# Attention's bias rows stored once and repeated from DRAM to DRAM in pieces of two heads, issued by GpSimd

## The chip, the cores and the metric

The kernel runs on one core of one Trainium2 chip. The metric is the time of one execution on the device in microseconds (us). A core has five engines with instruction queues of their own: TensorE (PE in the profile; its weight loads are PEld), VectorE (DVE), ScalarE (ACT), GpSimd (POOL) and SyncE (SP), and sixteen DMA engines that all queues share. SyncE, ScalarE and GpSimd issue transfers.

## The reference

One decoder layer over 2048 tokens of width 1024: a projection feeds eight RWKV-7 heads and eight heads of dilated attention, then an output product with layer norm, a mixture of 32 experts and a gated embedding with a second layer norm. The change concerns the attention's bias:

```python
def dilated_branch(q, k, v, rel_bias, window, dil):
    blk = window // dil                                  # 128 for each of the three patterns
    rel = np.arange(blk)[:, None] + blk - np.arange(2 * blk)[None, :]
    valid = ((rel >= 0) & (rel <= blk))[None] & (kpos >= 0)[:, None, :]
    bias = jnp.transpose(rel_bias[t5_bucket(np.clip(rel, 0, None) * dil)], (2, 0, 1))
    logits = jnp.einsum('bdhnqc,bdhnkc->bdhnqk', qs, kb) * (HEAD_DIM ** -0.5) + bias[None, None, :, None]
    logits = jnp.where(valid, logits, NEG_INF)
    ...
```

For a head and a pattern the bias of query i and key j depends only on i - j, so it is one row of 384 numbers, read with a shift of one for each query.

## The kernel before

The stages run one behind the other: `project` (the projection and what RWKV needs of it), `mixers` (RWKV and attention, woven together), `mix_out`, `route`, `ple`, `experts`, `finish`. The change lies in `attn_bias` (L953), a generator that `project` calls forward.

**What attn_bias makes.** For each of the three patterns GpSimd loads `hot` (which bucket each offset has, 32 x 384), the 32 x 8 table of `rel_bias` and `br` (8 x 384: the mask) (L960 to L962). A matmul (L965) looks the bias up for the eight heads, VectorE takes it from the mask (L966), and `br` then holds one row of 384 numbers for each head, in eight partitions. One transfer on ScalarE's queue (L967) writes each row 128 times to DRAM, into `biasrow` of 8 heads x 3 patterns x 128 x 384. In `attn_streams`, `load_bias` (L1002, SyncE) reads from there a tile in which row i is shifted by i, twelve times in all. `br` and `hot` have one buffer each, so the next pattern's loads wait until their readers are through.

**The loop in which it stands.** `project` holds TensorE's order by hand (`manual_schedule`); the other engines' order comes from a scheduler. The stretch is the loop over four column blocks `cc` and four token blocks `tb` (L478 to L486), in which every step does the same:

- `key(cc, tb)`: a product of 24 matmuls (L198 to L200) into one of five PSUM banks. ScalarE scales it into `sh` (L285), VectorE makes `o` (L287), SyncE stores `o` (L290), ScalarE squares `o` (L458).
- `value` twice: 24 shorter matmuls each. ScalarE copies the result into `ov` (L452), SyncE stores it to `va` (L453).
- between the two values `norm`: one matmul (L462) sums the square over each head. VectorE and ScalarE take the root and the reciprocal (L463 to L466), and SyncE stores the scaled key `rn` (L468).
- `next(bias)`: one yield of `attn_bias`.

`sh` and `ov` share the tag `"a"` of the pool `st`, which has two buffers, and are taken in the order `sh`, `ov`, `ov`. So a step's `sh` gets the buffer of the first `ov` of the step before, and L285 waits until its store to `va` has read it:

```python
sh = st.tile([P, BT + 1], F32, name="sh", tag="a")      # L283, in channels()
o = st.tile([P, 256], F32, name="ov", tag="a")          # L451, in value()
nc.scalar.copy(o, ps)
nc.sync.dma_start(self.va[t * P:(t + 1) * P, half * 256:(half + 1) * 256], o)
```

Behind L285 come L287, L458 and, in TensorE's fixed order, L462 with all that follows it. At the fourth step of a column block ScalarE also splits the next block's weights (L1230).

Four yields per pattern place the matmul of the patterns in steps 2, 6 and 10 of the loop, with the store behind it.

Of the kernel before, what the change touches and what calls it, by code (L numbers as in the profile page):

```python
# [18 lines left out]
P = 128  # L19
# [148 lines left out]
class K:  # L168
# [784 lines left out]
    def attn_bias(self, tile, bank):  # L953

        nc, I = self.nc, self.I
        L = 3 * P
        self.biasrow = rows = self.scratch("biasrow", (8, 3, P, L))
        for n in range(3):
            hot, br = tile(32, L + 8, "hot"), tile(8, L, "br")
            nc.gpsimd.dma_start(hot[:, 0:L], I["hot"][:, n])  # L960
            nc.gpsimd.dma_start(hot[:, L:], I["rel_bias"])
            nc.gpsimd.dma_start(br, I["gone"][:, n])  # L962
            yield
            ps = bank()
            nc.tensor.matmul(ps[0:8, 0:L], hot[:, L:], hot[:, 0:L], start=True, stop=True)  # L965
            nc.vector.tensor_tensor(out=br, in0=br, in1=ps[0:8, 0:L], op=ALU.subtract)  # L966
            nc.scalar.dma_start(rows[:, n], br.unsqueeze(1).to_broadcast([8, P, L]))  # L967
            yield
            yield
            yield  # L970

    def attn_open(self, es):
        self.al, self.ap = (es.enter_context(self.tc.tile_pool(name=name, bufs=1, reuse_waits="tile")) for name in ("al", "ap"))
# [1029 lines left out]
```

## Time and profile before

| | |
|---|---|
| median of three runs | 3235.52 us (3225.38 to 3244.79) |
| the profiled execution | 3237.51 us, of which the profile's span is 3235.7 us |
| VectorE busy | 2105.4 us (65%) |
| ScalarE busy | 1544.1 us (48%) |
| GpSimd busy | 628.3 us (19%) |
| TensorE's mean granted clock | 0.930 of full speed |
| moved by DMA | 533.09 MB, mean 165 GB/s |

Times within the span are counted from its start. A wait names an engine's instruction and what released it. [...] Transfers of SyncE and ScalarE have an issue time but no landing in the trace; those of GpSimd have both.

### The profile page before, as it was taken

Reading aid. Unit: us, or ns where it says so; the run is one execution under the profiler, and the core shown is the slowest. Engines: PE = TensorE matmul, PEld = TensorE weight load, DVE = VectorE, ACT = ScalarE, POOL = GpSimd, SP = SyncE. Lnnn points to the kernel's source line nnn. Section 1 sums busy time; section 2 is a strip of 40 time slices with the busy share of each in tenths; the row PEclk is TensorE's granted clock in tenths of the full one; section 3 lists DMA queues with packets and bytes.
Section 4 is the critical chain, followed back from the end, with each engine's and each line's share of the span. In section 5 each row is a group of like instructions: output and inputs, shape, how many; then the busy total and the mean of one; then the engine's idle time right before and its main releaser. Section 6 shows DMA issues by size and latency. Waiting matters only on the chain. (4 is left out here: it accounts for less than half of the span.)

```text
span 3235.7 us, 49913 instructions
## 1 busy us (share of the span) xinstructions
PE 2923.7 (90%) x17038; PEld 2331.5 (72%) x17039; DVE 2105.4 (65%) x4706; ACT 1544.1 (48%) x3704; POOL 628.3 (19%) x666
## 2 busy tenths in 40 slices
PE   7989888999799998999999799899999999999780
PEld 6666777777687777777787577788777777776560
DVE  4997333687564755656757678653577877775855
ACT  3444211465354454544544333311477777775754
POOL 0442000244110311211202122223011111111210
PEclk9999989999799888988997899999999999999895
DMA  5212433688725334235214453233499999997856
GB/s 172 76 56 95 104 89 79 197 276 265 160 62 109 112 81 113 83 83 117 81 29 134 143 179 131 98 129 100 165 295 314 327 311 311 327 299 236 284 155 214
DMA packets 364064, 533.09 MB, mean 165 GB/s; under 512 B 92376, under 2 KB 204640, under 8 KB 363792
## 3 DMA queue, kind: packets, MB, share of 16 engines
q1 hardware_dynamic: 330144, 459.09, 44.4%
q0 software_dynamic: 14496, 45.93, 6.0%
q10 hardware_dynamic: 19168, 24.86, 3.1%
q8 instruction: 136, 2.23, 0.3%
q14 instruction: 120, 0.98, 0.1%
HBM read 402.27 MB, written 128.06 MB: 164 GB/s over the span
## 5 line engine op out<-in xcount | busy, mean ns | idle before, releaser
L1711 DVE TENSOR_TENSOR wl<-raw,wh 128x512 fp32r<-128x512 f32 x768 | 478.3, 682 | 86.9 <-ACT wh L1710 86.5
L1710 ACT CAST wh<-raw 128x512 fp32r<-128x512 f32 x768 | 417.7, 621 | 12.9 <-DMA raw<-in_w_up_dram 10.0
L198 PE MATMUL ps<-xh,wh 128*128 128x512 f32 x640 | 261.3, 408 | 1.0 <-ACT xh L322 0.9
L199 PE MATMUL ps<-xl,wh 128*128 128x512 f32 x640 | 257.1, 402 | 1.2 <-DVE xl L323 1.2
L200 PE MATMUL ps<-xh,wl 128*128 128x512 f32 x640 | 256.6, 401 | 0.0
L1088 ACT ACTIVATE pe<-pe,ms 128x256 f32<-128x256 f32 (+1 forms) x384 | 174.9, 457 | 158.2 <-DVE ms L1085 144.7
L1840 POOL DMA_INDIRECT acc<-ysb,ix x48 | 95.1, 1981 | 622.1 <-ACT ysb L1839 401.4
L198 PE MATMUL pe<-wh,XX 128*128 128x512 f32 x480 | 198.8, 414 | 4.2 <-ACT wh L1710 4.2
L199 PE MATMUL pe<-wl,XX 128*128 128x512 f32 x480 | 191.1, 398 | 2.6 <-DVE wl L1711 2.6
L200 PE MATMUL pe<-wh,XX 128*128 128x512 f32 x480 | 189.9, 396 | 0.0
L198 PEld LDWEIGHTS ps<-xh,wh 128*128 128x128 f32 x640 | 123.9, 194 | 34.2 <-issue 2.8
L199 PEld LDWEIGHTS ps<-xl,wh 128*128 128x128 f32 x640 | 123.9, 194 | 29.8 <-DVE xl L323 2.4
L200 PEld LDWEIGHTS ps<-xh,wl 128*128 128x128 f32 x640 | 123.2, 192 | 29.2
L1094 PE MATMUL pl<-eye,pe 128*128 128x128 f32 x600 | 128.4, 307 | 13.7 <-ACT pe L1088 13.0
L1069 PE MATMUL pl<-KK,Q 128*128 128x256 f32 x432 | 117.4, 398 | 19.4 <-DMA KK<-ks 13.7
L1108 PE MATMUL po<-pe,V 128*64 128x128 f32 x1200 | 124.4, 313 | 8.5 <-DVE O L1122 6.7
L198 PE MATMUL pb<-gh,XH 128*128 128x512 f32 x320 | 126.4, 395 | 0.0
L199 PE MATMUL pb<-gl,XH 128*128 128x512 f32 x320 | 125.6, 393 | 0.0
L200 PE MATMUL pb<-gh,XL 128*128 128x512 f32 x320 | 125.4, 392 | 0.0
L1755 PE MATMUL pe<-wh,XX 128*128 128x512 f32 x288 | 119.9, 416 | 5.4 <-ACT wh L1710 5.4
L1756 PE MATMUL pe<-wl,XX 128*128 128x512 f32 x288 | 118.4, 411 | 2.9 <-DVE wl L1711 2.9
L1085 DVE CUSTOM_DVE_ANT_0 pe<-pl,bias 128x256 f32<-128x256 f32 x216 | 82.7, 419 | 56.4 <-PE pl L1069 38.6
(424 smaller groups left out, 7560.4 us busy)
## 6 DMA issues: line engine op xcount, KB each, us to landing
raw<-in_w_gate_dram SPq DMA_DIRECT2D x128, 512.0 KB
raw<-in_w_up_dram SPq DMA_DIRECT2D x128, 512.0 KB
raw<-in_w_down_dram SPq DMA_DIRECT2D x128, 512.0 KB
pk<-pk SPq DMA_DIRECT2D x32, 512.0 KB
pk_t<-pk SPq DMA_DIRECT2D x32, 512.0 KB
KK<-ks SPq DMA_DIRECT2D x64, 256.0 KB
wr<-in_w_in_dram SPq DMA_DIRECT2D x48, 256.0 KB
rkk<-rkk SPq DMA_DIRECT2D x32, 384.0 KB
```

Of the source, the lines that this page charges most:

```text
L198: mm(out, lh, rh, start=first, stop=False)
L199: mm(out, lh, rl, start=False, stop=False)
L200: mm(out, ll, rh, start=False, stop=last)
L1069: mm(pl[:, h], q, toks(KK[:, m, h], n, prev, 2), start=m == 0, stop=m == 1)
L1088: nc.scalar.activation(pe[:, h, w], pe[:, h, w], AF.Exp, bias=m_[h], scale=-1.0, accum_out=s_[h])
L1094: nc.tensor.transpose(pt[:, h, b], pe[:, h, b * P:(b + 1) * P], self.c("eye"))
L1108: mm(o[h * 64:(h + 1) * 64, j], vb[:, h * 64:(h + 1) * 64], tt[:, h, b], start=b == kb[0], stop=b == 1)
L1710: nc.scalar.copy(wh[:, c], raw[:, c])
L1711: nc.vector.tensor_tensor(out=wl[:, c], in0=raw[:, c], in1=wh.bitcast(F32)[:, c], op=ALU.subtract)
L1755: mm(ps, L[:, 0:P], wh, start=first, stop=False)
L1756: mm(ps, L[:, 0:P], wl, start=False, stop=last)
L1840: nc.gpsimd.indirect_dma_start(out=self.acc, out_offset=bass.IndirectOffsetOnAxis(ap=ix[0:r, e, b:b + 1], axis=0), in_=ysb[0:r], in_offset ...
```

## The change

A row of each head and pattern is first stored once (`biasone`, 8 x 3 x 384, 12 KB per pattern). Then four transfers per pattern, two heads each, read it from DRAM and write each row 128 times into `biasrow`. All five are issued by GpSimd, the old one by ScalarE. The number of yields per pattern is still four.

```diff
         self.biasrow = rows = self.scratch("biasrow", (8, 3, P, L))
+        one = self.scratch("biasone", (8, 3, L))
         for n in range(3):
...
             nc.vector.tensor_tensor(out=br, in0=br, in1=ps[0:8, 0:L], op=ALU.subtract)
-            nc.scalar.dma_start(rows[:, n], br.unsqueeze(1).to_broadcast([8, P, L]))
+            nc.gpsimd.dma_start(one[:, n], br)
             yield
-            yield
-            yield
+
+            for h in range(0, 8, 2):
+                nc.gpsimd.dma_start(rows[h:h + 2, n], one[h:h + 2, n].unsqueeze(1).to_broadcast([2, P, L]))
+                if h % 4:
+                    yield
```

In the built program TensorE, VectorE and SyncE have the same instructions in the same order as before, and ScalarE has them without the three stores. Lines from L958 on have other numbers in the changed kernel: by 1 up to its L967 (the subtraction), by 4 behind the loop. `hot`, `rel_bias` and `gone` are the loads of a pattern, `Lx` is the first work of the RWKV preparation behind the loop.

GpSimd, from the end of the token-shift work to the RWKV preparation, before:

```order
L363 TENSOR_TENSOR d<-X 128x512
L960 DMA hot<-in_hot_dram 32x384
L961 DMA hot<-in_rel_bias_dram 32x8
L962 DMA br<-in_gone_dram 8x384
L960 DMA hot<-in_hot_dram 32x384
L961 DMA hot<-in_rel_bias_dram 32x8
L962 DMA br<-in_gone_dram 8x384
L960 DMA hot<-in_hot_dram 32x384
L961 DMA hot<-in_rel_bias_dram 32x8
L962 DMA br<-in_gone_dram 8x384
L595 TENSOR_TENSOR Lx<-L 128x2x128
```

The same place of the changed kernel:

```order
L962 DMA hot<-in_rel_bias_dram 32x8
L968 DMA biasone<-br 8x384
L972 DMA biasrow<-biasone 2x128x384 x4
L963 DMA br<-in_gone_dram 8x384
L961 DMA hot<-in_hot_dram 32x384
L962 DMA hot<-in_rel_bias_dram 32x8
L968 DMA biasone<-br 8x384
L972 DMA biasrow<-biasone 2x128x384 x4
L963 DMA br<-in_gone_dram 8x384
L968 DMA biasone<-br 8x384
L972 DMA biasrow<-biasone 2x128x384 x4
L595 TENSOR_TENSOR Lx<-L 128x2x128
```

Each pattern's store and its four copies now stand in GpSimd's queue ahead of the next pattern's `br`.

ScalarE, around the first pattern's store, before:

```order
L464 ACTIVATE sq<-sq 128x512
L452 COPY ov<-ps 128x256
L967 DMA biasrow<-br 8x128x384
L285 ACTIVATE sh<-ps,prm 128x512
L458 ACTIVATE sq<-o,prm 128x512
```

The same place of the changed kernel:

```order
L464 ACTIVATE sq<-sq 128x512
L452 COPY ov<-ps 128x256
L285 ACTIVATE sh<-ps,prm 128x512
L458 ACTIVATE sq<-o,prm 128x512
L452 COPY ov<-ps 128x256
```

Only the store has left ScalarE's queue.

## Rows read from the trace of the kernel before

**Rows 1.** The page: busy time, share of the span and instructions of each engine.

```profile
PE 2923.7 (90%) x17038; PEld 2331.5 (72%) x17039; DVE 2105.4 (65%) x4706; ACT 1544.1 (48%) x3704; POOL 628.3 (19%) x666
```

**Rows 2.** Waits, 300 to 560 us: waiter <- releaser: total us, times, longest us.

```profile
POOL br L962 <- DMA biasrow<-br: 71.7, 2, 35.9
...
PE pn L462 <- ACT sq L458: 36.4, 3, 12.2
...
ACT sh L285 <- DMA va<-ov: 31.7, 3, 10.7
```

**Rows 3.** Windows from L462 to L462: us, busy by engine, clock, DMA share, GB/s.

```profile
378.01:402.42 24.41, 12.30 (x77) 10.56 (x75) 6.72 (x7) 3.93 (x7) 0.00 (x0) 0.82 0.51 78
402.42:417.00 14.58, 14.58 (x74) 12.49 (x75) 5.67 (x6) 2.79 (x5) 0.52 (x1) 0.83 0.36 108
442.27:466.61 24.34, 12.29 (x77) 10.56 (x75) 6.72 (x7) 3.93 (x7) 0.00 (x0) 0.84 0.51 79
466.61:481.49 14.88, 14.88 (x74) 12.79 (x75) 5.67 (x6) 2.79 (x5) 0.52 (x1) 0.81 0.38 113
...
506.70:531.22 24.52, 12.30 (x77) 10.56 (x75) 6.72 (x7) 3.93 (x7) 0.00 (x0) 0.84 0.51 77
531.22:546.20 14.98, 14.98 (x74) 12.89 (x75) 5.67 (x6) 2.80 (x5) 0.00 (x0) 0.80 0.36 112
...
558.33:570.46 12.13, 12.13 (x77) 10.60 (x76) 5.62 (x6) 2.79 (x5) 0.00 (x0) 1.00 0.18 65
570.46:583.12 12.66, 12.29 (x77) 10.55 (x75) 6.77 (x7) 3.89 (x8) 0.00 (x0) 1.00 0.25 79
```

**Rows 4.** The same view of the first long step, cut where TensorE stops.

```profile
378.01:390.20 12.19, 12.19 (x76) 10.55 (x74) 4.04 (x2) 2.52 (x5) 0.00 (x0) 1.00 0.53 82
390.20:402.42 12.22, 0.11 (x2) 0.01 (x1) 2.68 (x5) 1.41 (x2) 0.00 (x0) 0.65 0.50 75
```

**Rows 5.** Timeline of ScalarE: start, us, instruction, [idle before <- releaser].

```profile
371.22 0.55 ACTq L967 DMA_DIRECT2D biasrow<-br  x1
...
398.91 0.69 ACT L285 ACTIVATE sh<-ps,prm 128x512 f32<-128x512 f32 x1 [10.52 <-DMA va<-ov]
...
580.75 0.68 ACT L285 ACTIVATE sh<-ps,prm 128x512 f32<-128x512 f32 x1
```

**Rows 6.** Timeline of SyncE's queue, the two stores of that step in one row.

```profile
378.65 7.40 SPq L453 DMA_DIRECT2D va<-ov  x2
```

**Rows 7.** Timeline of GpSimd.

```profile
406.67 0.52 POOL L962 DMA_DIRECT2D br<-in_gone_dram  x1 [35.82 <-DMA biasrow<-br]
434.08 0.52 POOL L960 DMA_DIRECT2D hot<-in_hot_dram  x1 [26.89 <-PE ps L965]
...
600.18 0.62 POOL L595 TENSOR_TENSOR Lx<-L 128x256 f32<-128x256 f32 x1 [128.69 <-DVE L L591]
```

**Rows 8.** DMA queues (packets, MB, share of 16 engines) and one issue (KB each).

```profile
q1 hardware_dynamic: 330144, 459.09, 44.4%
q0 software_dynamic: 14496, 45.93, 6.0%
...
biasrow<-br ACTq DMA_DIRECT2D x3, 1536.0 KB
```

**Rows 9.** Timeline of VectorE.

```profile
367.37 3.35 DVE L466 RECIPROCAL rn<-sq 128x512 f32<-128x512 f32 x1 [0.70 <-ACT sq L464]
...
370.65 0.53 DVE L966 TENSOR_TENSOR br<-br,ps 8x384 f32<-8x384 f32 x1
```

**Rows 10.** GpSimd's issues: `br` in the DMA view (us to landing), slot tables (ns min/median/max).

```profile
br<-in_gone_dram POOLq DMA_DIRECT2D x3, 12.0 KB, 2.4
...
L1643 POOL DMA_DIRECT2D sl<-slotlist x4: 584/1298/1778, 2230.4 to 2239.0; - x4
```

**Rows 11.** The instructions of L1002: ns min/median/max, first and last start.

```profile
L1002 SPq DMA_DIRECT2D bias<-biasrow x12: 360/371/537, 813.2 to 1558.4; - x12
```

## The prediction

> **What bounds the kernel now.** TensorE is busy 2923.7 of 3235.7 us [rows 1], so time is won where it stands still or runs at a low clock. The change touches only the place where the attention bias is written, so I read that stretch: first who waits for whom between 300 and 560 us [rows 2]. TensorE has one wait worth naming there: three times, 36.4 us in all, its matmul L462 waits for ScalarE's square. Just above stands the reason: ScalarE's L285 waits three times for `va<-ov`, a store of 128 KB that holds a buffer of the tag that L285 writes next. And GpSimd waits twice for `biasrow<-br`, 35.8 us each.
>
> Next the stretch cut at each start of L462 on TensorE [rows 3]. A step of this loop takes 12.13 us (558.33 to 570.46), and the fourth step of a column block takes 12.66 (570.46 to 583.12). But the fourth steps that follow a bias store take 24.41, 24.34 and 24.52 us, and the steps after them 14.58, 14.88 and 14.98. In [rows 4] the first long step is cut in two: until 390.20 TensorE is full, then it does nothing for 12.2 us. The DMA share is 0.50 in that half, where a normal step has 0.18: eight of sixteen DMA engines are held. The store's eight heads take one engine each. After the idle time the step at 402.42 has a granted clock of 0.83: 17% of 14.58 us is 2.5 us, just what this step is longer than 12.13. [...]
>
> The order of events is in the timelines. The bias store is issued at 371.22 [rows 5] and lets `br` go at 406.67 [rows 7]: 35.45 us for 1536 KB [rows 8], 44 GB/s, 5.5 GB/s for each of eight engines. `va` is issued at 378.65 [rows 6] and L285, which waits for it, starts at 398.91 [rows 5], so `va` landed 20 us after its issue, when 27.7 of 35.45 us (78%) of the bias store were over.
>
> **What the losses are worth.** Long steps against 12.66: 11.75 + 11.68 + 11.86 = 35.29 us. Steps behind them against 12.13: 2.45 + 2.75 + 2.85 = 8.05 us. Together **43.3 us**, the most that the change can give back here.
>
> **The change part by part.** *Removed:* three issues on ScalarE's queue, 0.27 to 0.55 us each, while ScalarE is busy 3.93 of 24.41 us [rows 3]: nothing. *Added:* for each of three patterns one store of 12 KB and four copies of 384 KB, all on GpSimd. The order of TensorE, VectorE, ScalarE and SyncE is otherwise the same. On GpSimd the next row behind the last copies is L595 at 600.18 [rows 7], with 128.69 us idle ahead of it; between the copies stand only small loads for the next pattern, and GpSimd now idles 26.89 us behind the second pattern's `br` load until that pattern's matmul [rows 7]. GpSimd's issues cost nothing while this cover stands. The wait added is that the first copy follows the landing of the 12 KB store, and only those loads queue behind it. The reader of the bias, L1002, first issues at 813.2 [rows 11], some 300 us after the third pattern.
>
> *The price of the copies* is the open term: the bytes are the same, but they are read from DRAM, where the old store read eight SBUF partitions. No long DRAM-to-DRAM copy is timed in this trace. Bounds from [rows 8], over 16 x 3235.7 = 51771 engine-us: q1 moves 459.09 MB in 44.4% of it, 20.0 GB/s per engine; GpSimd's own queue q0 moves 45.93 MB in 6.0%, 14.8 GB/s; the old bias store 5.5 GB/s. For 1.573 MB on eight engines these hold the engines for 9.8, 13.3 and 35.4 us. I take **13.3**: it is the queue that the copies use, and a source of many rows in DRAM is more like its traffic than like eight partitions of SBUF. On sixteen engines it would be half.
>
> *Does `va` then land in time?* VectorE's subtraction L966 ends at 370.65 + 0.53 = 371.2 [rows 9]. Issue of the 12 KB store 0.5 us and landing 2.4 us, as for the load of the same size [rows 10], then 0.7 us for the first copy's issue: copies run from about 374.8. With the same 78% `va` lands at 374.8 + 0.78 x 13.3 = 385.2. It is needed when L285 starts in an undisturbed fourth step: 580.75 [rows 5] is 10.29 us behind that step's start, so 378.01 + 10.29 = 388.3. **It lands 3 us early and the stall is gone**, and with it the stretch at the low clock. The limit is a hold of (388.3 - 374.8) / 0.78 = 17.3 us; of each us above it 0.78 us come back as stall, and then about 2.7 us of clock per bias.
>
> *The issues.* Four loads of a slot table, the nearest issues on GpSimd with many pieces, take 0.58 to 1.78 us each [rows 10]. At 1.78 the last copy comes 7.1 us after the first; should it hold `va` as the first does, `va` lands at 392.3, 4.0 us late: 3 x (4.0 + 2.7) = 20 us lost again. This is the far end for this case.
>
> [...]
>
> **Sum.** 3237.5 us for the profiled execution (span 3235.7, 1.8 around it) - 43.3 = 3194.2. The median of the three runs is 2.0 below the profiled execution: **3192 us**. Everything behind 583 us starts 43 us earlier in the same order.
>
> **Rivals.**
> *The engines are held as long as before.* The price may lie in writing 3072 short rows to DRAM rather than in the source; then the hold stays 35.4 us and begins 3.6 us later, `va` lands at 402.4, and three stalls grow by 3.5 us: 3235.5 + 10.6 = 3246, within what can be told from no change. For it: the write side is unchanged. Against it: q1's mean of 20 GB/s includes many stores. [...]
> *A part of the stall stays,* with a hold between 17.3 and 31 us. At 25 us `va` is 6.0 us late: 3 x (6.0 + 2.7) = 26 us are lost again, 3218.
> *Two engines carry all four copies* (the slower side). A copy of two heads can use two engines, as eight heads used eight. Should all four land on the same two, 1.573 MB at 2 x 14.8 GB/s holds these for 53.1 us; `va` needs them too and lands 374.8 + 41.4 = 416.2, 17.3 us later than now, three times: 3287. It decides from a hold of 30.9 us, 25 GB/s per engine, above both measured rates; at 20.0 it is 3255. Against it: nothing in the trace shows that GpSimd's queue prefers certain engines. [...]
>
> **How the numbers follow.** A difference below 0.5% (16 us) can't be told from no change here, since the three runs span 19 us. Stall gone 0.76 (its own range 3180 to 3212: the runs' spread below, the issues' far end above); a part left 0.09; held as before 0.08; two engines 0.07. Faster by over 0.5% means below 3219: 0.76 and half of the second, 0.81. Slower by over 0.5% is the two-engine case, 0.07. The rest, 0.12, is within. The range is 3179 to 3224: the first case and most of the second.
>
> **What would show it.** Right: L462 waits for ScalarE once, below 1 us; all fourth steps near 12.7 us and those behind near 12.1 at clock 1.00; L285 waits for no `va`; `br`'s second load waits for the 12 KB store only, a few us. The copies' hold shows in the DMA share of the steps: about 0.5 more for some 13 us. Wrong: long steps remain (held as before, or two engines, told apart by a share raised by 0.50 or by 0.13), or the steps are short and the time is lost behind 583 us.

## The result, and the profile after

The changed kernel takes **3195.79 us** (median of six runs, 3188.58 to 3220.28), the kernel before 3238.43 in the runs beside it: a ratio of **0.9879 [0.9851, 0.9908]** with its 95% interval (taken over all runs, so not quite the quotient of the medians, 0.9868). The forecast was 3192. The profiled span is 3192.6 us against 3235.7.

The page of the changed kernel, busy time by engine, answers to [rows 1]:

```profile
span 3192.6 us, 49926 instructions
...
PE 2910.0 (91%) x17038; PEld 2320.6 (73%) x17039; DVE 2098.2 (66%) x4706; ACT 1541.6 (48%) x3704; POOL 641.5 (20%) x681
```

The kernel is 43 us shorter with the same matmuls. To see where, the span of each kernel is cut at the first and the last L462 of the loop (columns as in [rows 3]: us; busy time of PE, PEld, DVE, ACT and POOL, each with its number of instructions; the granted TensorE clock as a share of full speed, a mean over the stretch; the mean busy share of the sixteen DMA engines; GB/s). Before:

```profile
352.80:583.12 230.32, 193.57 (x1119) 165.73 (x1117) 89.99 (x97) 47.69 (x85) 3.08 (x6) 0.91 0.35 81
583.12:3235.70 2652.58, 2417.70 (x14626) 1928.67 (x14626) 1759.31 (x4236) 1354.86 (x3379) 526.22 (x588) 0.93 0.58 180
```

After, with two of the three fourth steps that follow a bias, one step behind and the last fourth step, from L462 to L462, which answer to [rows 3]:

```profile
354.10:541.34 187.24, 185.77 (x1118) 159.62 (x1116) 90.10 (x97) 47.01 (x85) 17.72 (x21) 1.00 0.32 100
541.34:3192.60 2651.26, 2408.90 (x14626) 1921.19 (x14626) 1752.16 (x4236) 1352.90 (x3379) 524.39 (x588) 0.93 0.58 180
...
379.32:391.97 12.65, 12.29 (x76) 10.55 (x74) 6.81 (x7) 3.88 (x8) 0.36 (x1) 1.00 0.66 188
391.97:404.20 12.23, 12.23 (x74) 10.70 (x75) 5.62 (x6) 2.63 (x5) 0.00 (x0) 1.00 0.33 108
...
479.52:492.18 12.66, 12.29 (x76) 10.56 (x74) 6.82 (x7) 3.88 (x8) 0.00 (x0) 1.00 0.64 188
...
528.68:541.34 12.66, 12.29 (x76) 10.55 (x74) 6.76 (x7) 3.88 (x8) 0.00 (x0) 1.00 0.26 84
```

The loop gave 230.32 - 187.24 = 43.08 us, the 2650 us behind it 1.3, and the part ahead of it takes 1.3 more. Its granted clock went from 0.91 to 1.00, and the bias still moves: GpSimd is busy 17.72 us in it instead of 3.08. The steps of 24.4 us are gone (the third fourth step not shown here takes 12.66), and a step with a bias behind it (share 0.66) takes as long as the one without (share 0.26). The waits between 300 and 560 us, in place of [rows 2]:

```profile
DVE sh L284 <- DMA va<-ov: 8.8, 3, 3.0
...
POOL biasrow L972 <- DMA biasone<-br: 4.6, 3, 1.5
...
PE pn L462 <- ACT sq L458: 1.5, 4, 0.4
```

L462 waits 1.5 us in all instead of 36.4. The store `va` is still waited for, by VectorE's small copy L284 into the same `sh`, but 3.0 us at most, with nothing late behind it. In the kernel before, that copy waited too:

```profile
DVE sh L284 <- DMA va<-ov: 46.3, 6, 15.2
```

GpSimd's timeline, the copies' row of the DMA view (last number: median us to landing) and SyncE's:

```profile
372.79 0.52 POOL L968 DMA_DIRECT2D biasone<-br  x1 [0.64 <-DVE br L967]
374.81 4.34 POOL L972 DMA_DIRECT2D biasrow<-biasone  x4 [1.50 <-DMA biasone<-br]
```

```profile
biasrow<-biasone POOLq DMA_DIRECT2D x12, 384.0 KB, 13.6
```

```profile
379.96 4.04 SPq L453 DMA_DIRECT2D va<-ov  x2
```

And VectorE's and ScalarE's rows that tell when `va` was in, and when it was needed:

```profile
388.06 0.15 DVE L284 COPY sh<-edge 128x1 f32<-128x1 f32 x1 [2.94 <-DMA va<-ov]
```

```profile
389.61 0.68 ACT L285 ACTIVATE sh<-ps,prm 128x512 f32<-128x512 f32 x1
```

The copies' first issue started at 374.81 and they took 13.6 us each (forecast 13.3). `va` landed at 388.06, 8.1 us after its issue instead of 20, and ScalarE's L285 used it at 389.61, 1.5 us later; 3.1 were forecast. But L285 isn't the first that needs it. In VectorE's queue stand L284, the scaling of `rn` (L467), the rest of the weights' split (L1235) and L287, in this order:

```profile
389.21 1.29 DVE L1235 TENSOR_TENSOR wl<-wr,wh 128x512 fp32r<-128x512 f32 x2 [0.34 <-ACT wh L1234]
390.42 0.74 DVE L287 SCALAR_TENSOR_TENSOR o<-ps,prm,sh 128x512 f32<-128x512 f32 x1
```

Only the 0.34 us that VectorE idles ahead of L1235 stand between a later `va` and a later L287, for which the square L458 and L462 wait. The margin is some 0.4 us, as experiment 10 shows.

### The profile page after: what moved, and what is told of

Read it like the earlier page. It is cut to its first block, busy times and chain, and to the rows that moved or that the text cites. A ratio compares the mean times of both kernels' runs of the same rounds, so it can differ in the third digit from the quotient of the medians.

```text
span 3192.6 us, 49926 instructions
## 1 busy us (share of the span) xinstructions
PE 2910.0 (91%) x17038; PEld 2320.6 (73%) x17039; DVE 2098.2 (66%) x4706; ACT 1541.6 (48%) x3704; POOL 641.5 (20%) x681
## 5 line engine op out<-in xcount | busy, mean ns | idle before, releaser
L1714 ACT CAST wh<-raw 128x512 fp32r<-128x512 f32 x768 | 417.3, 620 | 12.4 <-DMA raw<-in_w_up_dram 10.4
L1098 PE MATMUL pl<-eye,pe 128*128 128x128 f32 x600 | 127.5, 306 | 12.4 <-ACT pe L1092 12.1
L1089 DVE CUSTOM_DVE_ANT_0 pe<-pl,bias 128x256 f32<-128x256 f32 x216 | 82.6, 419 | 49.7 <-PE pl L1073 36.4
```

What stands on the lines that cost most here:

```text
L1098: nc.tensor.transpose(pt[:, h, b], pe[:, h, b * P:(b + 1) * P], self.c("eye"))
L1714: nc.scalar.copy(wh[:, c], raw[:, c])
```

## The experiments

The change does three things at once: GpSimd issues instead of ScalarE, the source is DRAM instead of SBUF, and one transfer becomes four. The theories: **source** (reading each row from DRAM makes the store quick), **issuer** and **pieces**. All ratios are against the kernel before, run on the same chip beside each. All but experiments 8 and 9 keep the engines' order apart from the edited transfers (in 6 and 11 a few of VectorE's instructions trade places; in 9 and 11 L467 comes ahead of L284). The *hold* is the time for which a bias transfer keeps its DMA engines.

### 1. The issuer alone

```diff
-            nc.scalar.dma_start(rows[:, n], br.unsqueeze(1).to_broadcast([8, P, L]))
+            nc.gpsimd.dma_start(rows[:, n], br.unsqueeze(1).to_broadcast([8, P, L]))
```

> Only the issuer changes: the old store of eight heads, read from eight SBUF partitions, is issued by GpSimd instead of ScalarE. Source theory (the price of a row lies in its eight-partition SBUF source): GpSimd's second load of br still waits 33 to 38 us, the three fourth steps stay at 22 to 27 us, and the time is that of the kernel before, ratio 0.995 to 1.005. Issuer theory (GpSimd's queue lets the store to va through): fourth steps of 12.7 us and a ratio near 0.988.

Measured: 1.0065 [1.0037, 1.0094], slower. First the window of the first fourth step, then the DMA view, SyncE, and ScalarE's L285:

```profile
378.04:409.86 31.82, 12.29 (x77) 10.55 (x75) 6.72 (x7) 3.98 (x8) 0.54 (x1) 0.75 0.49 70
```

```profile
biasrow<-br POOLq DMA_DIRECT2D x3, 1536.0 KB, 35.3
```

```profile
378.68 7.14 SPq L453 DMA_DIRECT2D va<-ov  x2
```

```profile
406.35 0.69 ACT L285 ACTIVATE sh<-ps,prm 128x512 f32<-128x512 f32 x1 [17.93 <-DMA va<-ov]
```

The store takes 35.3 us as before, so the issuer gave nothing of the gain. It costs something: `va` landed at 406.35, just ahead of the bias store's end, and not at 398.91 [rows 5]. The three fourth steps (31.82, 31.14, 31.20) are 20.9 us longer in sum than in [rows 3], which is the 0.65%; neither theory had this loss.

### 2. The source alone

```diff
-            nc.scalar.dma_start(rows[:, n], br.unsqueeze(1).to_broadcast([8, P, L]))
+            nc.gpsimd.dma_start(one[:, n], br)
             yield
+            nc.scalar.dma_start(rows[:, n], one[:, n].unsqueeze(1).to_broadcast([8, P, L]))
...
```

> Only the source changes: the 12 KB are stored once, and one transfer of eight heads, issued by ScalarE, repeats them from DRAM to DRAM. Source theory: eight engines are held for 10 to 14 us instead of 35, the fourth steps take 12.6 to 13 us, ratio 0.985 to 0.990. Issuer theory: fourth steps of 22 to 27 us, ratio near 1.000. Pieces theory (transfers of two heads let the store to va in between them): also near 1.000.

Measured: 0.9878 [0.9818, 0.9939], the whole gain. The window of the first fourth step, SyncE's store, and VectorE's L284:

```profile
377.96:390.62 12.66, 12.29 (x76) 10.56 (x74) 6.82 (x7) 3.88 (x8) 0.00 (x0) 1.00 0.45 157
```

```profile
378.61 4.04 SPq L453 DMA_DIRECT2D va<-ov  x2
```

```profile
384.51 0.15 DVE L284 COPY sh<-edge 128x1 f32<-128x1 f32 x1 [0.75 <-DMA va<-ov]
```

With ScalarE as issuer and eight heads in one transfer, `va` is in after 5.9 us and the stall is gone. ScalarE's queue (q10 in the DMA view) has its last packets of the bias before 385.1, a hold of 11.9 us from the issue at 373.18. The rival "held as before", by which the writing of short rows sets the price, falls: the rows written are the same.

### 3. The pieces alone

The old source, in four transfers of two heads by GpSimd:

```diff
-            nc.scalar.dma_start(rows[:, n], br.unsqueeze(1).to_broadcast([8, P, L]))
...
+            for h in range(0, 8, 2):
+                nc.gpsimd.dma_start(rows[h:h + 2, n], br[h:h + 2].unsqueeze(1).to_broadcast([2, P, L]))
...
```

> Issuer and pieces change, the source does not: four transfers of two heads, issued by GpSimd, read from br in SBUF. Source theory: the hold stays 33 to 38 us, fourth steps of 22 to 27 us, ratio 0.995 to 1.005. Pieces theory: fourth steps near 12.7 us, ratio near 0.988.

Measured: 1.0070 [1.0041, 1.0099]. Fourth steps 31.84, 35.17 and 31.74 us. The first, and the DMA view:

```profile
377.56:409.40 31.84, 12.29 (x76) 10.56 (x74) 6.72 (x7) 3.93 (x7) 0.00 (x0) 0.73 0.51 64
```

```profile
biasrow<-br POOLq DMA_DIRECT2D x12, 384.0 KB, 39.4
```

A quarter of the bytes, read from two partitions, takes 39.4 us while the others run beside it. The pieces theory falls from this side. Hold and steps lie above what the source theory gave; the steps are near those of experiment 1, with the same issuer.

### 4. One piece, otherwise as changed

```diff
-            for h in range(0, 8, 2):
-                nc.gpsimd.dma_start(rows[h:h + 2, n], one[h:h + 2, n].unsqueeze(1).to_broadcast([2, P, L]))
+            nc.gpsimd.dma_start(rows[:, n], one[:, n].unsqueeze(1).to_broadcast([8, P, L]))
```

> As the changed kernel, but one transfer of eight heads per pattern instead of four of two. Source theory: landing after 12 to 17 us, fourth steps of 12.6 to 13 us, ratio 0.985 to 0.990, the same as the changed kernel. Pieces theory: the store to va waits behind the one large transfer, fourth steps above 15 us, ratio above 0.991.

Measured: 0.9887 [0.9857, 0.9917], fourth steps 12.66 us. DMA view, SyncE and VectorE:

```profile
biasrow<-biasone POOLq DMA_DIRECT2D x3, 1536.0 KB, 12.4
```

```profile
377.86 4.04 SPq L453 DMA_DIRECT2D va<-ov  x2
```

```profile
385.20 0.15 DVE L284 COPY sh<-edge 128x1 f32<-128x1 f32 x1 [2.18 <-DMA va<-ov]
```

The pieces theory falls from this side too. All 1536 KB land in 12.4 us, and this is the plain price that the forecast put at 13.3.

### 5. Why SBUF was slow: the same rows, spread over partitions

The source stays in SBUF and ScalarE issues one transfer, but the heads stand in partitions 0, 4, ... 28 instead of 0 to 7 (the matmul then has 32 output rows, and GpSimd first clears what the loads leave unwritten).

```diff
-            nc.tensor.matmul(ps[0:8, 0:L], hot[:, L:], hot[:, 0:L], start=True, stop=True)
+            nc.tensor.matmul(ps[0:32, 0:L], hot[:, L:], hot[:, 0:L], start=True, stop=True)
...
-            nc.scalar.dma_start(rows[:, n], br.unsqueeze(1).to_broadcast([8, P, L]))
+            nc.scalar.dma_start(rows[:, n], br[0:32:4].unsqueeze(1).to_broadcast([8, P, L]))
```

> The source stays SBUF and ScalarE issues one transfer as before, but the eight heads lie in partitions 0, 4, 8 to 28 instead of 0 to 7. Partition-group theory (the old store was slow because eight neighbouring partitions share a narrow way out): the hold falls to 9 to 15 us, fourth steps near 12.7 us, ratio 0.985 to 0.990. Rival (each engine is slow because all its rows come from one partition): the hold stays 33 to 38 us and the ratio is 0.995 to 1.005. [...]

Measured: 0.9841 [0.9781, 0.9902]. ScalarE's issue, the release of `br` on GpSimd, and the fourth step:

```profile
373.58 1.28 ACTq L969 DMA_DIRECT2D biasrow<-br  x1
```

```profile
384.57 0.41 POOL L961 MEMSET br<- 32x384 f32 x1 [11.42 <-DMA biasrow<-br]
```

```profile
380.40:393.06 12.66, 12.29 (x77) 10.55 (x75) 6.77 (x7) 3.88 (x8) 0.93 (x2) 1.00 0.35 124
```

The hold is 11.0 us instead of 35.45, with the bytes, rows and issuer unchanged. So "SBUF against DRAM" was not the cause either: eight *neighbouring* partitions were. With the heads four partitions apart the store runs at 143 GB/s instead of 44, 3.2 times the rate. Why neighbouring partitions are slow was not shown.

### 6. The wait moved: buffers of its own for `ov`

The old store is left alone; `ov` gets two buffers outside tag `"a"` (lines behind it move by one).

```diff
-                        o = st.tile([P, 256], F32, name="ov", tag="a")
+                        o = vo.tile([P, 256], F32, name="ov", tag="v")
```

> The bias store stays as in the kernel before; instead ov gets two buffers of its own, so that L285 waits for no store to va (sq has one buffer less, to make room). Buffer theory (the stall comes only through the shared tag): the hold stays near 35 us, the fourth steps fall to 12.6 to 14 us, ratio 0.985 to 0.991. Rival (the held engines stop TensorE in other ways too, by the stores of o and rn or the weight loads): fourth steps above 18 us, ratio above 0.993.

Measured: 0.9903 [0.9880, 0.9926]. Waits between 340 and 600 us, and the fourth step with the one behind:

```profile
POOL br L963 <- DMA biasrow<-br: 73.3, 2, 36.6
ACT ov L453 <- DMA va<-ov: 46.9, 9, 8.4
```

```profile
376.83:389.49 12.66, 12.29 (x76) 10.55 (x74) 6.75 (x6) 3.83 (x7) 0.00 (x0) 1.00 0.54 88
389.49:404.65 15.16, 12.40 (x75) 10.66 (x75) 5.76 (x6) 2.59 (x5) 0.00 (x0) 1.00 0.53 95
```

The engines are held as long as before (GpSimd waits 36.6 us for the bias store, 35.9 in [rows 2]), yet most of the loss is gone. That shows the chain: it ran through the shared buffer, from `va` to L285. The rest waits at `ov`'s own buffer: steps behind of 15.16, 15.14 + 13.76 and 14.89 + 13.84 us are 12.1 us above five times 12.13, and 43.3 - 12.1 = 31.2 us is 0.96%, where 0.97% was measured.

### 7. All sixteen engines

Each row is stored twice, and one GpSimd transfer per pattern repeats sixteen rows 64 times. The first two dimensions of `biasrow` and `biasone` trade places for it.

```diff
-            nc.gpsimd.dma_start(one[:, n], br)
+            nc.gpsimd.dma_start(one[n], br.unsqueeze(1).to_broadcast([8, 2, L]))
...
+            nc.gpsimd.dma_start(rows[n].rearrange("h (t i) l -> (h t) i l", t=2), one[n].rearrange("h t l -> (h t) l").unsqueeze(1).to_broadcast([16, P // 2, L]))
```

> As the changed kernel, but each row is stored twice and one transfer with an outer dimension of sixteen repeats it, so that sixteen engines can share it. Engine-count theory (an engine moves 15 GB/s, so the hold goes with the rows of one engine): landing after 6 to 9 us instead of 13.5, the store to va lands 2 to 5 us after its issue instead of 8, and the ratio is again 0.985 to 0.990, since no stall was left. Rival (DRAM is the limit): landing still 12 to 15 us.

Measured: 0.9876 [0.9853, 0.9899]. Windows of 2 us (last columns: clock, DMA share, GB/s):

```profile
379.00:381.00 2.00, 2.00 (x20) 2.00 (x19) 1.30 (x2) 0.63 (x1) 0.00 (x0) 1.00 0.96 327
381.00:383.00 2.00, 2.00 (x14) 1.73 (x13) 2.00 (x1) 0.37 (x1) 0.00 (x0) 1.00 0.28 97
```

The engines are full until 381 and then free: the share from 374.8 to 381 is 0.87, at 291 GB/s. So the hold falls to some 6 us, and DRAM wasn't the limit at 12.4. `va` is in by 383.60, 5.1 us after its issue at 378.52 (5.5 in the second pattern). No time comes of it. With the stall gone there is nothing left to gain here, as the forecast's bound of 43.3 us says.

### 8. The four pieces, issued by ScalarE

```diff
-                nc.gpsimd.dma_start(rows[h:h + 2, n], one[h:h + 2, n].unsqueeze(1).to_broadcast([2, P, L]))
+                nc.scalar.dma_start(rows[h:h + 2, n], one[h:h + 2, n].unsqueeze(1).to_broadcast([2, P, L]))
```

> The four DRAM-to-DRAM copies of two heads are issued by ScalarE instead of GpSimd. The order of the mixers' stage changes in this build, so the steps of the loop decide, not the total. Two-engine theory (this queue puts all four copies on the same two engines): the DMA share rises by about 0.13 for some 50 us per pattern, and fourth steps take 30 to 45 us. Eight-engine theory: share up by 0.5 for 10 to 14 us, fourth steps of 12.6 to 13 us.

Measured: 1.0073 [1.0050, 1.0095], slower, but not by the expected route. A window while TensorE stands still, the long step, and ScalarE's timeline:

```profile
381.00:385.00 4.00, 0.00 (x0) 0.00 (x0) 0.00 (x0) 0.00 (x0) 0.00 (x0) 0.50 0.13 50
...
364.74:393.29 28.55, 13.25 (x78) 10.71 (x77) 5.98 (x7) 2.84 (x6) 2.03 (x4) 0.78 0.19 66
```

```profile
376.07 16.40 ACTq L972 DMA_DIRECT2D biasrow<-biasone  x2
392.52 0.72 ACT L458 ACTIVATE sq<-o,prm 128x512 f32<-128x512 f32 x1 [15.77 <-issue]
```

Here all copies do go over two engines: a share of 0.13 is 2 of 16, at 50 GB/s, 25 per engine. The changed kernel's share in its fourth steps is 0.66, so GpSimd's copies spread. But the loss is not `va`'s. ScalarE is kept 16.4 us in issuing two copies, and its next square, for which L462 waits, comes late: the third steps take 28.55, 27.68 and 28.67 us. The loop is 10.4 us longer than before (240.7 against 230.3); of the 23.7 us measured, the other 13 lie behind it, where the program has another order in the mixers' stage, and stay unexplained.

### 9. Twice the hold, by ScalarE

Experiment 2 with a second such transfer into a tensor that nobody reads.

```diff
             nc.scalar.dma_start(rows[:, n], one[:, n].unsqueeze(1).to_broadcast([8, P, L]))
+            nc.scalar.dma_start(more[:, n], one[:, n].unsqueeze(1).to_broadcast([8, P, L]))
```

> One transfer of eight heads from DRAM by ScalarE, as in the run that changes the source alone, and a second one just like it into a DRAM tensor that nobody reads: the hold is doubled on the same eight engines. The order of the mixers' stage changes in this build, so the steps of the loop decide. Hold theory (the store to va lands when about 78% of the hold is over, as in the kernel before): a hold of some 24 us from about 374, va lands near 393, fourth steps of 16 to 19 us. Rival (the low price of the source alone decides, not how long the engines are held): fourth steps of 12.6 to 13 us.

One run of 3213.97 us (before: 3250.14), with another order in the mixers' stage, so only the loop is read. The first fourth step; ScalarE's queue q10 in the DMA view of 392 to 393.4 us (it has no row in that of 393.4 to 400); and VectorE:

```profile
378.00:390.77 12.77, 12.40 (x75) 10.66 (x75) 6.84 (x7) 3.72 (x8) 0.00 (x0) 1.00 0.63 229
```

```profile
q10 hardware_dynamic: 87, 0.12, 23.7%
```

```profile
384.62 0.15 DVE L284 COPY sh<-edge 128x1 f32<-128x1 f32 x1
```

The engines are held until about 393.4, some 21 us from the first issue at 372.23, where experiment 2 held them 11.9. `va` is in by 384.62, as in experiment 2; the fourth steps take 12.77, 12.76 and 12.76 us. By the forecast's "78% of the hold" it would have landed near 389, too late. The steps ahead of them take 14.10, 14.86 and 13.41 us instead of 13.09: ScalarE's second issue takes 2.0 to 3.4 us, and L285 stands behind it.

### 10. Twice the load, by GpSimd

Each copy of the changed kernel is issued twice, the second into a tensor that nobody reads, so that a pattern's copies can reach all sixteen engines.

```diff
                 nc.gpsimd.dma_start(rows[h:h + 2, n], one[h:h + 2, n].unsqueeze(1).to_broadcast([2, P, L]))
+                nc.gpsimd.dma_start(more[h:h + 2, n], one[h:h + 2, n].unsqueeze(1).to_broadcast([2, P, L]))
```

> The changed kernel with each copy of two heads issued twice, the second time into a DRAM tensor that nobody reads: eight copies per pattern on GpSimd's queue instead of four. Cursor theory (successive transfers of this queue move on to other engines): the eight copies lie on all sixteen engines, the DMA share of the fourth steps rises to 0.9 or more, each copy still lands after 13 to 16 us, va lands a little later than in the changed kernel, fourth steps of 12.6 to 16 us. Rival (the eight copies share eight engines): share about 0.65 for twice the time, later copies land after 20 us or more, fourth steps of 20 to 26 us and a ratio near 0.998.

Measured: 0.9906 [0.9881, 0.9931]. The first fourth step, the DMA view and VectorE in that step:

```profile
377.95:390.90 12.95, 12.29 (x76) 10.55 (x74) 6.73 (x7) 3.88 (x8) 4.63 (x5) 1.00 0.86 225
```

```profile
biasrow<-biasone POOLq DMA_DIRECT2D x12, 384.0 KB, 15.5
```

```profile
387.42 0.15 DVE L284 COPY sh<-edge 128x1 f32<-128x1 f32 x1 [3.67 <-DMA va<-ov]
...
388.15 1.28 DVE L1236 TENSOR_TENSOR wl<-wr,wh 128x512 fp32r<-128x512 f32 x2
389.35 0.74 DVE L287 SCALAR_TENSOR_TENSOR o<-ps,prm,sh 128x512 f32<-128x512 f32 x1
```

The share is 0.86, a little less than expected. The copies land in 15.5 us, and the fourth steps are 12.95, 13.12 and 13.20 us. L285 starts on time in the first of them (388.24, 10.29 us behind its L462, as undisturbed); late is VectorE's queue behind L284. L284 starts 9.47, 9.63 and 9.71 us behind its L462, and the steps are 0.29, 0.46 and 0.54 us above 12.66, so `va` is needed 9.2 us behind L462. In the changed kernel L284 starts at 8.7 to 8.8: a margin of some 0.4 us. This run is just past it. With the steps behind, the loop takes 190.58 us, 3.3 more than in the changed kernel.

### 11. Twice as long on the same engines, by GpSimd

Experiment 4, each row written 256 times; the reader takes the first 128.

```diff
-            nc.gpsimd.dma_start(rows[:, n], one[:, n].unsqueeze(1).to_broadcast([8, P, L]))
+            nc.gpsimd.dma_start(rows[:, n], one[:, n].unsqueeze(1).to_broadcast([8, 2 * P, L]))
```

> One transfer of eight heads from DRAM, issued by GpSimd, that writes each row 256 times instead of 128 (the reader takes the first 128): 256 rows for each of eight engines instead of 128, at the low price. Whole-hold theory (on GpSimd's queue the store to va lands only when the bias is through, as in the run where only the issuer changed, 406.35 against 406.8): landing after 23 to 26 us, va lands near 397, fourth steps of 20 to 24 us and the steps behind them of 14 to 15, ratio 0.994 to 1.000. Rival (as on ScalarE's queue, where a hold twice as long left the fourth steps at 12.77 us: va passes after a number of rows, however many follow): fourth steps of 12.6 to 13.5 us, ratio 0.985 to 0.990.

Measured: 0.9872 [0.9836, 0.9907]. DMA view, fourth step, SyncE and VectorE:

```profile
biasrow<-biasone POOLq DMA_DIRECT2D x3, 3072.0 KB, 22.2
```

```profile
376.07:388.73 12.66, 12.29 (x77) 10.55 (x75) 6.91 (x7) 3.89 (x8) 0.00 (x0) 1.00 0.63 232
```

```profile
376.71 4.04 SPq L453 DMA_DIRECT2D va<-ov  x2
```

```profile
384.26 0.15 DVE L284 COPY sh<-edge 128x1 f32<-128x1 f32 x1 [1.60 <-DMA va<-ov]
```

A hold of 22.2 us costs nothing: `va` is in 7.5 us after its issue, as behind 12.4 us. So what is queued behind the rows that `va` meets did not count here.

### 12. The changed kernel once more

> The changed kernel once more beside the runs of this job: ratio 0.985 to 0.991, fourth steps of 12.7 us, copies landing after 13 to 14 us.

Measured: 0.9865 [0.9838, 0.9892], fourth steps 12.66, 12.67 and 12.66 us. No experiment beats it: 2, 4, 5, 7 and 11 all have intervals that overlap this one.

## Why the prediction was right, and where not

- **What bounds, and the 43.3 us: right.** The chain bias store, `va`, shared buffer, L285, L462 was read from waits and windows, and experiment 6 shows its middle by cutting it. The loop gave 43.08 us; neither a long stall nor a stretch at the low clock is left in it. In the kernel before, the clock was 1.00 in the window from 382 to 390 us, 0.50 from 398 to 406, when TensorE had idled since 390.20, and 0.89 on average from 406.8 to 410: the stall costs its own time and a stretch at 0.50 behind it. That the eight heads of the store kept eight engines fits what was measured: a share of 0.50 with eight [rows 4], of 0.13 with two (experiment 8), of 0.87 with sixteen rows at a time (experiment 7, other traffic included).
- **Price of the copies: right** (13.3 us taken; 13.6 per copy, 12.4 in one piece), in part by luck: the mean of all of GpSimd's transfers had no tie to such copies, which ran at 25 GB/s per engine on two engines (experiment 8). The reason given was only half right: many rows in DRAM are quick, but so are eight SBUF partitions that stand apart (11.0 us).
- **Start of the copies and the issues: right.** The first issue starts at 374.81; with its 1.1 us, and less the 1.3 us by which this loop starts later, that is 374.6 against 374.8. An issue takes about 1.1 us (4.34 for four), not 1.78.
- **"It is needed when L285 starts": not the first that needs it.** VectorE's L284 waits for the same buffer, and L287 stands behind it. `va` is needed 9.2 us behind the step's start (experiment 10), not 10.29: by 387.2 in the forecast's times, not 388.3. The limit of the hold becomes (387.2 - 374.8) / 0.78 = 15.9 us, and of the 3.1 us forecast 2.0 are left. The measured margin is 0.4.
- **"With the same 78% `va` lands at 385.2" and "the limit is a hold of 17.3 us": the step that failed.** It scaled `va`'s landing with the whole hold. The copies start 1.1 us apart, so the engines are in fact held until about 374.8 + 3 x 1.1 + 13.6 = 391.7, near that limit; `va` came 1.6 us later than forecast, counted from a loop that starts 1.3 us later (388.06 against 385.2 + 1.3). In the changed kernel alone, 78% of the last copy's time would fit as well (374.8 + 3.3 + 0.78 x 13.6 = 388.7). But experiments 9 and 11 have holds of about 21 and 22.2 us, beyond the limit, and fourth steps of 12.66 to 12.77.
- **In its place, as far as counts go: the price of one row.** Divide `va`'s time from issue to landing by the bias's time per row on an engine. Before: 20.3 us by 35.45/128 = 0.277 us, 73 rows. After: 8.1 by 13.6/128, 76. Experiment 2: 5.9 by 11.9/128, 63. Experiment 3: `va` issued at 378.20 and in at 405.90, 27.7 by 39.4/128, 90. Experiment 4: 7.3 by 12.4/128, 76. Experiment 10: `va` issued at 378.59 and in at 387.42, 8.8 by 15.5/128, 73. Experiment 11: 7.5 by 22.2/256, 87. So `va` lets some 63 to 90 bias rows pass; in experiment 11 some 110 more followed (9.5 of the 22.2 us were still to come). Experiment 1 stands apart: 27.7 by 0.276, 100 rows, up to the end of the bias store. `va` has 387.2 - 378.65 = 8.5 us, so with 73 to 87 rows a row may cost some 0.10 to 0.12 us; at 0.121 experiment 10 just fails. Two things stay open: every row here has 1536 bytes, so a price per row and one per byte can't be told apart, and no trace here shows how a DMA engine chooses between two queues.
- **The rivals.** "Held as before" fell to experiments 2 and 4. "A part stays" did not happen, and its range (holds of 17.3 to 31 us) was priced by the step that failed. "Two engines" did not happen on GpSimd's queue (a share of 0.64 to 0.66 in its fourth steps, against 0.13 on two engines); where it was forced (experiment 8), the rate was 25 GB/s per engine, the very rate at which this rival comes out even with the kernel before, and the loss came from ScalarE's issuing, which no rival had.
- **A gap among GpSimd's issues,** in experiment 10 alone: the seventh issue (379.90 to 380.97) takes 1.07 us like the others, while the eighth starts only at 385.39, with 4.4 us idle ahead of it (5.0 and 4.8 in the other patterns). What held it is open.
- **Two of its sums.** Four issues of 1.78 us put the last copy's issue 3 x 1.78 = 5.3 us behind the first, not 7.1. And the 2.7 us of clock that a late `va` was to cost each time did not come with a small delay: in experiment 10 `va` was late by 0.3 to 0.5 us, and the clock stayed at 1.00. Neither sum is in the 3192.

## What to carry to other kernels

Where an engine waits for a small store, look at what shares its DMA engines at that moment, and price that transfer per row (of 1536 bytes here, of which `va` let 63 to 90 pass, 100 in experiment 1), not by its whole length: a broadcast store from eight neighbouring partitions was slow by its source here (35.45 us), and either a copy from DRAM (11.9 us in experiment 2) or rows that stand four partitions apart (11.0 us) cured it. A transfer on the same engines that was long but quick per row delayed `va` little (holds of about 21 and 22.2 us in experiments 9 and 11, `va` in 7.5 us after its issue in the latter); behind the slow one it landed 20 us after its issue. Ask which engine's queue meets the late store first: the margin here was set by a small copy on VectorE, not by the large instruction on ScalarE. Change the issuing engine only with its cost in view: ScalarE was kept from its work by issuing (16.4 us for two copies in experiment 8, 2.0 to 3.4 us for the second one in experiment 9), and the slow SBUF store delayed `va` more when GpSimd issued it (27.7 us from issue to landing in experiments 1 and 3, against 20.3).

## What was not expected of the hardware

- The same SBUF store, issued by GpSimd instead of ScalarE, held `va` 7.4 us longer (406.35 against 398.91) at the same 35.3 us. The packed traces of the kernels before and after show one difference between the queues: ScalarE's moved the old store in packets of 1536 bytes, one row each (1024 for a pattern), GpSimd's moves the copies nearly all in packets of 4608 bytes, three rows each (336 for a pattern). Whether that has to do with it was not tested.
- ScalarE was kept 16.4 us by issuing two 384 KB copies that run on two engines. GpSimd issued four in 4.34 us.
- Rows of 1536 bytes from DRAM to DRAM ran at 25 GB/s per engine on two engines, and at 1.573 MB / 12.4 us / 8 = 15.9 on eight; the second counts issue and landing and has other traffic beside it.
